# Placing split weights 4,224 bytes apart, with sets aside by 0, 64 or 96 bytes, in a one-core encoder layer

## The chip, the cores and the metric

The kernel runs on one core of one Trainium2 chip. The metric is the device time of one execution in microseconds. Three executions of the kernel before were timed; their median counts. One more execution was profiled: its trace holds the start of every instruction on each engine, the DMA packets and the semaphore events, but no addresses.

## The reference

One encoder layer over 512 positions of width 1,024, in float32:

```python
h = modulate(rmsnorm(x, norm_ffn1), sh1, sc1)
x = x + 0.5 * g1 * swiglu(h, w_ffn1_in, w_ffn1_out)      # inner width 2816
h = modulate(rmsnorm(x, norm_mix), sh2, sc2)
qa, ka, va, qb, kb, vb, ga, gb = split(h @ w_in)
ya = window_gqa_sink(rope(norm(qa)), rope(norm(ka)), va, sink_a) @ w_branch_a
yb = subln(diff_attention(rope(norm(qb)), rope(norm(kb)), vb, lam)) @ w_branch_b
x = x + g2 * ((sigmoid(ga) * ya + sigmoid(gb) * yb) @ w_out)
h = modulate(rmsnorm(x, norm_ffn2), sh3, sc3)
x = x + 0.5 * g3 * swiglu(h, w_ffn2_in, w_ffn2_out)
```

The nine vectors sh, sc and g are `silu(c) @ w_mod + b_mod`.

## The kernel before

**Precision.** Every large product is made in three matmuls of the type fp32r. Both factors are split into a high part (the value rounded to fp32r, by ScalarE) and a low part (the rest, by VectorE); `split_from` (line 190) does this. The three are high x high, high x low and low x high: `mm3` (lines 174 to 176), and `two` (lines 443 to 445), which does it for two column blocks of 256 moving columns. `first_products` (681), `project` (1125 to 1127) and `project_pairs` (1144 to 1146) issue the same three; in the last two the roles are exchanged, so that the weights are the moving operand and the hidden state is loaded into the array.

**Where weights lie.** A weight tile arrives by DMA in a `raw` tile (four buffers) and is split into a set: a high part of 128 x 1,024 in the tile `high` and a low part in the tile `low`. Each of these has five places (`HILO`) of 1,024 columns (4,096 bytes per partition); `high_low` hands them out in turn and skips those that are held. With `aside` a set begins some columns after the start of its place. Before, the columns are: 0 by default; 16 (`ASIDE`, 64 bytes) for the sets of the seven-product units (`Unit.prepare`), `project_pairs`, gate 5, two sets of `w1i`, most sets of branch A and the last two of the mix; 64 (`FAR`) for the second matmul of FFN 1 (`Out1.prepare`); 8 (`STEP`) and 56 (`STEP_1`) for one set each. A set of 1,024 columns with 16 aside reaches 16 columns into the next place. Some units keep weights elsewhere: `apart` sets in a `b8` tile, three gates in `u4` tiles.

**The moving side.** Hidden states and activations lie split in tiles `b8` (4 x 512 columns; twelve buffers) and `u4` (2 x 512; six buffers).

**Stages, in order.** (1) FFN 1 up: `first_products` with 512 moving columns, then plain pairs from `w1i`, then units of seven products instead of eight (`Unit`, a Strassen-like scheme, 256 moving columns). Four times between them `Out1` makes the second matmul for a chunk of the inner width (512 columns). (2) A boundary that makes the last four sets of `Out1` by halves of the sequence (256 columns) while the next norm is made, with three gates. (3) Projections of the two attentions, the attentions themselves, the remaining gates beside them, the two branches; branch A by halves (256 columns). (4) The mix `w_mix`: six sets with 512 columns, then two by halves. (5) FFN 2: a plain unit, then units, each two 256 wide.

**What sets the order.** In FFN 1 and FFN 2 `run_items` writes the order out, with due times for loads (`ASK`) and splits (`MAKE`), and a split is only made when a place is free. In the attentions a planner (`Line`) orders pieces by their costs. TensorE, VectorE and ScalarE follow that written order in the boundaries and in the first stage; elsewhere the framework orders them by their dependencies. Weight DMAs are issued by SyncE, additions to weights in memory (`accum_op`) by GpSimd.

**Addresses.** A tile's place in memory follows from the order in which the kernel first asks for its name; sizes are rounded up to 32 bytes. Before that order is: `half`, 24 `sm`, `ones`, `ident`, `par`, 8 `x`, `high`, six `mod`, `low`, three `mod`, `sub8`, `lam_s`, `nlam`, `begin`, `ka`, 12 `b8`, `ccol`, 6 `u4`, `pos`, 4 `raw`, 8 `f2`, then small ones up to nearly the end of the memory. `half` stands at byte 4,224.

Of the kernel before, what the change touches and what calls it, by code (L numbers as in the profile page):

```python
# [11 lines left out]
F32 = mybir.dt.float32  # L12
F32R = mybir.dt.float32r
I32 = mybir.dt.int32
# [4 lines left out]
P = 128  # L19
D = 1024  # L20
T = 512
NC = D // P
NT = T // P
# [73 lines left out]

RAW, HILO, F2 = 4, 5, 8

ASIDE = 16  # L100

FAR = 64


STEP, STEP_1 = 8, 56
BRANCH_ASIDES = (STEP, ASIDE, ASIDE, ASIDE), (ASIDE, ASIDE, 0, 0)
MIX_ASIDES = 0, 0, 0, 0, 0, 0, ASIDE, ASIDE

CHUNKS = (range(0, 6), range(6, 12), range(12, 16), range(16, 22))
PLAIN, LAST_1 = 3, 4  # L110
# [24 lines left out]
def layer(ctx: ExitStack, tc: tile.TileContext, a: dict):  # L135
# [31 lines left out]
    def keep(shape, nm, dt=F32):  # L167
        return sb.tile(shape, dt, name=nm, tag=nm, bufs=1)
# [28 lines left out]
    def high_low(n=1024, aside=0, holder=None):  # L197
        while turn[0] % HILO in holders:
            turn[0] += 1
        i = turn[0] % HILO  # L200
        turn[0] += 1
        if holder:
            holders[i] = holder
        i = i * 1024 + aside
        return tuple(t[:, i : i + n] for t in parts)

    def let_go(holder):
# [16 lines left out]
    half = keep([P, 8], "half")  # L224
    V.memset(half, -0.5)
    S.activation(small(8), half, AF.Silu)
    ones = keep([P, P], "ones")
    V.memset(ones, 1.0)
    ident = keep([P, P], "ident")
    make_identity(nc, ident)  # L230

    par = keep([P, NPAR], "par")
    x = [xt() for _ in range(NC)]
    parts, modv = [], []
    for nm, n in (("high", 6), ("low", 9)):
        parts.append(keep([P, HILO * 1024 + ASIDE], nm, F32R))
        modv += [keep([P, NC], f"mod{v}") for v in range(len(modv), n)]
    sub8, lam_s, nlam = (keep([P, n], nm) for nm, n in (("sub8", 1), ("lam_s", 2), ("nlam", 1)))

    def mod_load(v, c, w=None):  # L240
        if w is None:
# [2 lines left out]
        return w  # L244


    begin, begins, norms = keep([P, 8 * NC], "begin"), {}, {SC1: NORM1, SC2: NORM2, SC3: NORM3}

    def mod_begin(v):
        if v in (SH1, SH2, SH3):  # L250
# [33 lines left out]
    class Norm:  # L284
# [41 lines left out]
        def sums(self, sq, r, first, last):  # L326
            if first:
                self.st[r.start] = bank("op" if r.start else "tp")
            for t in range(r.start // P, r.stop // P):
                i = 2 * (t - r.start // P)  # L330
                PE.matmul(
                    self.st[r.start][:, i : i + 2], sq[:, t * P : (t + 1) * P], ones[:, 0:2],
                    start=first and i == 0, stop=last and (t + 1) * P == r.stop, skip_group_check=True,
                )

# [111 lines left out]
    class Unit:  # L447
# [12 lines left out]
        MAKE = {"s1": 5, "a11": 3, "a12": 2, "s2": 4, "s4": 2, "s3": 2, "a22": 3}  # L460
        asked, length = ("s1", "a11", "a12", "a22"), 1.0

        in_order = ()
        spare, roomy, apart, more = ("s1",), (), (), {"s1": ("s2", "a11"), "s2": ("s4", "a12"), "a11": ("s3", "a21")}

        def place(self, q):
# [14 lines left out]
        def prepare(self, q):  # L481

            if q in self.ready:
                return
            self.ask(q)
            n = self.depth * 2 * P
            if q in self.apart:
                both = b8().rearrange("p a b -> p (a b)")
                hi, lo = both[:, 0:n], both[:, 1024 : 1024 + n]
            else:  # L490
                hi, lo = high_low(n, ASIDE, (self, q))
            t = self.at[q]
            with tc.issue_after(copied[0]) if q in self.in_order and copied else nullcontext():
                split_from(hi, lo, t)
            self.ready[q] = hi, lo
            if q in self.more:
                s, src = self.more[q]
                G.dma_start(t, self.srcs[src], accum_op=ALU.add)
                self.at[s] = t
# [101 lines left out]

    cact = [sbuf("ka", [P, D], F32, 1)]
    hh, hl = new_h()
    ccol = keep([P, 3 * NC], "ccol")[:, 0:NC]
    nc.scalar.dma_start(ccol, a["c"])
    tc.keep_in_program_order(nc.scalar.dma_start(par, a["par"]))
    for c in range(NC):
# [2 lines left out]
    with tc.manual_schedule(engines=BOUND | {mybir.EngineType.SP, mybir.EngineType.Pool}):  # L610
# [14 lines left out]
                start=j == 0, stop=j == 3, skip_group_check=True,  # L625
            )
        warm(3)
        w1, pos = {}, []

        def first_loads(k):  # L630
            scale = mod_load(SC1, k)
            if k == 0:
                pos.append(keep([P, NT], "pos", I32))
            shift = mod_load(SH1, k) if k == 0 else None
            raw = sbuf("raw", [P, 1024], F32, RAW)
            nc.sync.dma_start(raw, a["w1s"][k])
            w1[k] = [scale, shift or mod_load(SH1, k), raw]
# [134 lines left out]
    rest, later, latest = rest[: EARLY * NC], rest[EARLY * NC : (EARLY + NEXT) * NC], rest[(EARLY + NEXT) * NC :]  # L772

    row = u4(F32).rearrange("p a b -> p (a b)")[:, 0:NROW]
    pos = pos[0]
    freq = keep([P, HD // 2], "freq")
    small_loads = [
        (row, a["row"].partition_broadcast(P)), (pos, a["pos"]), (freq, a["freq"].partition_broadcast(P)),
# [54 lines left out]
    class Out1:  # L833
# [17 lines left out]
        def prepare(self, m):  # L851
            if m not in self.ready:
                self.ask(m)
                aside = FAR if not self.by_halves(m) else STEP_1 if m == NC - LAST_1 else ASIDE
                if self.final and m == 0:
                    while turn[0] % HILO != 1:
                        turn[0] += 1
                t = self.ready[m] = high_low(self.depth * P, aside, (self, m))
                with tc.issue_after(copied[0]):
                    split_from(*t, self.at[m])  # L860
# [52 lines left out]
    with tc.manual_schedule(engines={mybir.EngineType.SP, mybir.EngineType.Pool}):  # L913
# [4 lines left out]
        for q in range(4, 2 * PLAIN):  # L918

            w, sums_from = loaded1, split[1]  # L920
            if q < 5:
                with tc.issue_after(split[0]), tc.issue_after(split[1]):
                    loaded1 = [load_split(a["w1i"][1, k], aside=ASIDE) for k in range(2)]
            behind = split[1]
            out = pair_banks()
            for k in range(NC):
                wh, wl = w[k // 4]
                for i in range(2):
                    o = (k % 4) * 256 + i * P
# [53 lines left out]
    V.tensor_scalar(sub8, par[:, SUBLN : SUBLN + 1], 1.0 - LAM_INIT, None, ALU.mult)  # L983

    NF = HD // 2
    posf = keep([P, NT], "posf")
    V.tensor_copy(posf, pos)
    tb = u4(F32)
    tb = [tb[:, i, :] for i in range(2)]
# [141 lines left out]
    def project_pairs(srcs, then):  # L1131

        n = 2 * P
        out = [bank("acc") for _ in range(2)]
        for u, src in enumerate(srcs):
            wh, wl = load_main(src, ASIDE)
            for t in range(NT):
                ht = slice(t * P, (t + 1) * P)
                po = out[t // 2][:, t % 2 * n : (t % 2 + 1) * n]
                for i in range(4):  # L1140
                    k = 4 * u + i
                    w = slice(i * n, (i + 1) * n)
                    first, last = k == 0 and t % 2 == 0, k == NC - 1 and t % 2 == 1
                    PE.matmul(po, hh[k][:, ht], wh[:, w], start=first, stop=False, skip_group_check=True)
                    PE.matmul(po, hh[k][:, ht], wl[:, w], start=False, stop=False, skip_group_check=True)
                    PE.matmul(po, hl[k][:, ht], wh[:, w], start=False, stop=last, skip_group_check=True)
                    yield MM3 / 2
        then(out)
# [11 lines left out]
    def gates(more=lambda: True):  # L1160
        while gate_next[0] < 16 and more():
            j = gate_next[0]
            gate_next[0] += 1

            wh, wl = load_main(a["w_gate"][j], ASIDE * (j == EARLY_A))
            out = bank("acc")
            for k in range(NC):
                o = k * P
                mm3(out, wh[:, o : o + P], wl[:, o : o + P], hh[k], hl[k], k == 0, k == NC - 1)
                yield MM3  # L1170
            gate_end(j, out)
# [71 lines left out]

    kb_h, kb_l, vb_h, vb_l, qb_h, qb_l = (b8() for _ in range(6))
    rqb = keep([P, NT, 8], "rqb")
    nrqb = keep([P, NT, 8], "nrqb")
    ob_h, ob_l = b8(), b8()
    done, turns = {"a": 0, "b": 0}, {"a": 0, "b": 0, "o": 0, "w": (0, 0), "q": 0, "t": 0}

# [143 lines left out]
    def tables_a():  # L1393
        late = u4(F32).rearrange("p a b -> p (a b)")
        nc.sync.dma_start(late, table_scr)
        table["qa"], table["ka"] = (four(late)[i : i + 2] for i in (0, 2))
        ka = sbuf("ka", [P, 2, T], F32R, 1)
        wa.update(k=(ka[:, 0, :], ka[:, 1, :]), rq=keep([P, NT, 8], "rqa"))

    def two_blocks(raw, nh, tabs, i, rs, scale8):  # L1400

# [211 lines left out]
    def main():  # L1613
# [30 lines left out]

        for i, r in enumerate(HALVES):
            line.drain(lambda: done["a"] >= 2 * i + 2)
            yield from branch(a["w_ya"], 0, *wa["o"], then_b, load_split, r, BRANCH_ASIDES[i])

    mix = []
    line.run(main())  # L1650
# [9 lines left out]
    nc.sync.dma_start(cact[0], c_scr.partition_broadcast(P))  # L1660
    mod_begin(G3)
    for m in range(NC):
        w = load_split(a["w_mix"][m], aside=MIX_ASIDES[m])

        def products(po, r, w=w):
            wh, wl = w
# [107 lines left out]
            V.scalar_tensor_tensor(g, g, -1.0, self.bank[1, t], ALU.mult, ALU.mult)  # L1774

    plain = units[0] = Plain(units[0].srcs, 4, h_operand, None, 0)
    lead = units[1]
    lead.spare, lead.roomy, lead.apart = ("s1", "a11", "a12"), ("a22",), ("s1", "a12")
    for u in units[1:]:
# [254 lines left out]
```

## Time and profile before

| | us |
|---|---|
| three timed executions | 1045.57, 1045.63, 1048.86 |
| their median | 1045.63 |
| the profiled execution | 1044.11 |
| its span, first to last instruction | 1042.3 |
| busy: matmuls (PE) | 1034.8 |
| busy: weight loads (PEld) | 953.2 |
| busy: VectorE (DVE) | 785.5 |
| busy: ScalarE (ACT) | 575.6 |
| busy: GpSimd (POOL) | 165.7 |

The ends of matmuls are modelled in the profile and overlap, so their busy time is no measure of their speed. How fast they follow each other is read from the starts in the timeline: the start of the last of a run less that of the first, by the count between them. A name such as `acc<-b,high` lists the tile that is written and the tiles that are read, buffer numbers left out (`b` is `b8`, `u` is `u4`). The granted clock of TensorE is 0.999 of full speed throughout.

### The profile page before, as it was taken

What the parts mean: (1) busy time and instruction counts of PE and PEld (TensorE: products, weight loads), DVE (VectorE), ACT (ScalarE), POOL (GpSimd) and SP (SyncE); (2) the same over time, 40 slices, a digit from 0 to 9 for tenths busy, and PEclk for the clock granted to TensorE, in tenths of its full rate; (3) what the DMA queues carried; (4) which work ended last, traced back from release to release, by engine and by line L of the source; (5) the groups of instructions that cost most, each with busy time, mean ns of one, the idle gap of its engine ahead of it and who ended that gap; (6) DMA issues with size and microseconds to landing.
All of it is one profiled execution on the core that took longest, in us unless ns stands there. A gap on an engine that the chain in (4) does not pass through costs nothing.

```text
span 1042.3 us, 18751 instructions
## 1 busy us (share of the span) xinstructions
PE 1034.8 (99%) x7348; PEld 953.2 (91%) x7348; DVE 785.5 (75%) x1436; ACT 575.6 (55%) x948; POOL 165.7 (16%) x190
## 2 busy tenths in 40 slices
PE   9999999999999999999999999999999999999998
PEld 6889899899998998899888888989999999999998
DVE  6886667567796679859772588976899777877867
ACT  6664335234454442667785855525867556655553
POOL 1101110110110100543333101001111111112110
PEclk9999999999999999999999999999999999999999
DMA  9977786966984459796646834974498998989874
GB/s 366 346 218 187 242 235 198 275 173 180 259 207 150 149 203 410 232 261 140 179 97 184 242 124 158 366 229 112 98 238 190 244 226 206 231 216 220 208 150 127
DMA packets 68793, 220.92 MB, mean 212 GB/s; under 512 B 8288, under 2 KB 10976, under 8 KB 68704
## 3 DMA queue, kind: packets, MB, share of 16 engines
q1 hardware_dynamic: 46224, 146.52, 38.7%
q0 software_dynamic: 19344, 68.70, 35.1%
q10 hardware_dynamic: 3136, 4.51, 1.2%
q8 instruction: 57, 0.93, 0.3%
q14 instruction: 32, 0.26, 0.1%
HBM read 209.46 MB, written 10.23 MB: 211 GB/s over the span
## 4 chain that ended last, share of the span: by engine, by line
PE 93%; DVE 3%; ACT 3%; issue 0%; DMA 0%; POOL 0%; DVEq 0%; ACTq 0%; POOLq 0%
PE acc L443 7%; PE acc L444 7%; PE acc L445 7%; PE sc L443 6%; PE sc L445 6%; PE sc L444 6%; PE sc L174 5%; PE sc L175 5%; PE sc L176 5%; PE acc L174 4%; PE acc L176 4%; PE acc L175 4%; PE acc L1125 2%; PE acc L1126 2%; PE acc L1127 2%; PE tp L1203 1%
## 5 line engine op out<-in xcount | busy, mean ns | idle before, releaser
L190 ACT CAST high<-raw 128x1024 fp32r<-128x1024 f32 (+2 forms) x160 | 155.9, 985 | 149.8 <-PE sc L175 37.7
L190 DVE TENSOR_TENSOR low<-raw,high 128x1024 fp32r<-128x1024 f32 (+2 forms) x160 | 181.3, 1141 | 49.4 <-ACT high L190 48.5
L443 PE MATMUL acc<-b,high 128*128 128x256 f32 x508 | 140.9, 277 | 0.0
L444 PE MATMUL acc<-b,high 128*128 128x256 f32 x508 | 140.7, 277 | 0.1
L445 PE MATMUL acc<-b,low 128*128 128x256 f32 x508 | 140.6, 277 | 0.0
L445 PE MATMUL sc<-b,low 128*128 128x256 f32 x500 | 138.5, 277 | 0.0
L443 PE MATMUL sc<-b,high 128*128 128x256 f32 x500 | 138.5, 277 | 0.0
L444 PE MATMUL sc<-b,high 128*128 128x256 f32 x500 | 138.4, 277 | 0.0
L190 DVE TENSOR_TENSOR low<-u,high 128x1024 fp32r<-128x1024 f32 (+1 forms) x73 | 87.5, 1200 | 21.8 <-ACT high L190 20.3
L190 ACT CAST high<-u 128x1024 fp32r<-128x1024 f32 (+1 forms) x73 | 75.4, 1036 | 49.1 <-PE sc L175 16.2
L174 PE MATMUL sc<-b,high 128*128 128x512 f32 (+1 forms) x272 | 97.5, 359 | 0.0
L175 PE MATMUL sc<-b,high 128*128 128x512 f32 (+1 forms) x272 | 97.3, 358 | 0.0
L176 PE MATMUL sc<-b,low 128*128 128x512 f32 (+1 forms) x272 | 97.1, 357 | 0.0
L444 PEld LDWEIGHTS acc<-b,high 128*128 128x128 f32 x508 | 95.5, 188 | 0.4 <-DVE b L1818 0.3
L443 PEld LDWEIGHTS acc<-b,high 128*128 128x128 f32 x508 | 95.5, 188 | 0.3 <-ACT f L520 0.2
L445 PEld LDWEIGHTS acc<-b,low 128*128 128x128 f32 x508 | 95.4, 188 | 0.0
L443 PEld LDWEIGHTS sc<-b,high 128*128 128x128 f32 x500 | 94.1, 188 | 0.2 <-ACT f L520 0.2
L445 PEld LDWEIGHTS sc<-b,low 128*128 128x128 f32 x500 | 93.9, 188 | 0.1
L444 PEld LDWEIGHTS sc<-b,high 128*128 128x128 f32 x500 | 93.9, 188 | 0.0
L174 PE MATMUL acc<-b,high 128*128 128x512 f32 (+1 forms) x240 | 89.4, 372 | 0.3 <-DVE u L190 0.3
L176 PE MATMUL acc<-b,low 128*128 128x512 f32 (+1 forms) x240 | 87.1, 363 | 0.0
L175 PE MATMUL acc<-b,high 128*128 128x512 f32 (+1 forms) x240 | 86.9, 362 | 0.0
(387 smaller groups left out, 2713.5 us busy)
## 6 DMA issues: line engine op xcount, KB each, us to landing
u<-w_mod SPq DMA_DIRECT2D x40, 512.0 KB, 8.0
b<-w_mod SPq DMA_DIRECT2D x32, 512.0 KB, 5.7
raw<-w2i SPq DMA_DIRECT2D x31, 512.0 KB, 5.3
u<-w2i POOLq DMA_DIRECT2D x31, 512.0 KB, 7.1
u<-w1u POOLq DMA_DIRECT2D x24, 512.0 KB, 7.4
raw<-w1u SPq DMA_DIRECT2D x24, 512.0 KB, 6.7
raw<-w1o SPq DMA_DIRECT2D x24, 384.0 KB, 4.3
raw<-w_gate SPq DMA_DIRECT2D x16, 512.0 KB, 4.2
```

The costliest lines, as they stand in the source:

```text
L174: PE.matmul(out, wh, xh, start=first, stop=False)
L175: PE.matmul(out, wh, xl, start=False, stop=False)
L176: PE.matmul(out, wl, xh, start=False, stop=last)
L190: last = S.copy(hi, src), V.tensor_tensor(lo, src, f(hi), ALU.subtract)
L443: PE.matmul(out, wh[:, s], xh, start=first and j == 0, stop=False, skip_group_check=True)
L444: PE.matmul(out, wh[:, s], xl, start=False, stop=False, skip_group_check=True)
L445: PE.matmul(out, wl[:, s], xh, start=False, stop=last and j == 1, skip_group_check=True)
L1125: PE.matmul(out[t][:, 0:n], hh[k][:, ht], wh[:, o : o + n], start=k == 0, stop=False)
L1126: PE.matmul(out[t][:, 0:n], hh[k][:, ht], wl[:, o : o + n], start=False, stop=False)
L1127: PE.matmul(out[t][:, 0:n], hl[k][:, ht], wh[:, o : o + n], start=False, stop=k == NC - 1)
L1203: PE.transpose(tp[:, j * P : (j + 1) * P], src, ident)
```

## The change

Places are 1,056 columns (`PLACE`, 4,224 bytes) apart instead of 1,024, so no set reaches into the next place. Sets stand aside by 0 columns where the moving side is 512 wide, by 16 (`NARROW`, 64 bytes) where it is 256 wide, and by 24 (`TURN`, 96 bytes) in a few sets: sets 4 and 5 of the last `Out1`, set 1 of branch A's first half, set 6 of the mix, and `a11` and `a21` of the plain unit in FFN 2. The two `w1i` sets and gate 5, with 512 moving columns, go from 16 to 0; the last two sets of branch A from 0 to 16; `Out1` from 64 to 0.

Memory is paid for elsewhere: `ones` has 2 columns instead of 128, `begin` 6 x 8 instead of 8 x 8, `ccol` 8 instead of 24; `nrqb` takes the buffer of `freq`, `rqa` that of `Ckb`. `sub8`, `lam_s`, `nlam`, `pos`, two of the `mod` tiles and `ccol` are asked for before `x`, one `mod` tile stands between `high` and `low` and three after `low`, three after `b8`. No product, split or DMA is added or taken away.

```diff
-ASIDE = 16
-FAR = 64
-STEP, STEP_1 = 8, 56
-BRANCH_ASIDES = (STEP, ASIDE, ASIDE, ASIDE), (ASIDE, ASIDE, 0, 0)
-MIX_ASIDES = 0, 0, 0, 0, 0, 0, ASIDE, ASIDE
+PLACE, NARROW, TURN = 1024 + 32, 16, 24
...
-        i = i * 1024 + aside
+        i = i * PLACE + aside
...
-    ones = keep([P, P], "ones")
+    ones = keep([P, 2], "ones")
...
+    sub8, lam_s, nlam = (keep([P, n], nm) for nm, n in (("sub8", 1), ("lam_s", 2), ("nlam", 1)))
+    pos = keep([P, NT], "pos", I32)
+    parts, modv = [], []
+    def mods(n):
+        modv.extend(keep([P, NC], f"mod{v}") for v in range(len(modv), n))
+    mods(2)
+    ccol = keep([P, NC], "ccol")
     x = [xt() for _ in range(NC)]
-    parts, modv = [], []
-    for nm, n in (("high", 6), ("low", 9)):
-        parts.append(keep([P, HILO * 1024 + ASIDE], nm, F32R))
-        modv += [keep([P, NC], f"mod{v}") for v in range(len(modv), n)]
+    for nm, n in (("high", 3), ("low", 6)):
+        parts.append(keep([P, (HILO - 1) * PLACE + 1024 + TURN], nm, F32R))
+        mods(n)
...
-    begin, begins, norms = keep([P, 8 * NC], "begin"), {}, {SC1: NORM1, SC2: NORM2, SC3: NORM3}
+    begin, begins, norms = keep([P, 6 * NC], "begin"), {}, {SC1: NORM1, SC2: NORM2, SC3: NORM3}
...
-        in_order = ()
+        in_order = turned = ()
...
-                hi, lo = high_low(n, ASIDE, (self, q))
+                hi, lo = high_low(n, TURN if q in self.turned else NARROW, (self, q))
...
-    ccol = keep([P, 3 * NC], "ccol")[:, 0:NC]
+    mods(9)
...
-                aside = FAR if not self.by_halves(m) else STEP_1 if m == NC - LAST_1 else ASIDE
+                aside = 0 if not self.by_halves(m) else TURN if m < NC - LAST_1 + 2 else NARROW
...
-                    loaded1 = [load_split(a["w1i"][1, k], aside=ASIDE) for k in range(2)]
+                    loaded1 = [load_split(a["w1i"][1, k]) for k in range(2)]
...
-            wh, wl = load_main(a["w_gate"][j], ASIDE * (j == EARLY_A))
+            wh, wl = load_main(a["w_gate"][j])
...
-    nrqb = keep([P, NT, 8], "nrqb")
+    nrqb = sbuf("freq", [P, NT, 8], F32, 1)
...
-        wa.update(k=(ka[:, 0, :], ka[:, 1, :]), rq=keep([P, NT, 8], "rqa"))
+        wa.update(k=(ka[:, 0, :], ka[:, 1, :]), rq=sbuf("Ckb", [P, NT, HD], F32, 1)[:, :, 0:8])
...
-            yield from branch(a["w_ya"], 0, *wa["o"], then_b, load_split, r, BRANCH_ASIDES[i])
+            yield from branch(a["w_ya"], 0, *wa["o"], then_b, load_split, r, [NARROW, NARROW if i else TURN, NARROW, NARROW])
...
-        w = load_split(a["w_mix"][m], aside=MIX_ASIDES[m])
+        w = load_split(a["w_mix"][m], aside=0 if m < NC - LAST else TURN if m == NC - LAST else NARROW)
...
+    plain.turned = ("a11", "a21")
```

More of the change, by code (lines that the diff above doesn't have):

```diff
@@ L232, in layer @@
     par = keep([P, NPAR], "par")
-    x = [xt() for _ in range(NC)]
-    parts, modv = [], []
-    for nm, n in (("high", 6), ("low", 9)):
-        parts.append(keep([P, HILO * 1024 + ASIDE], nm, F32R))
-        modv += [keep([P, NC], f"mod{v}") for v in range(len(modv), n)]
-    sub8, lam_s, nlam = (keep([P, n], nm) for nm, n in (("sub8", 1), ("lam_s", 2), ("nlam", 1)))
+    sub8, lam_s, nlam = (keep([P, n], nm) for nm, n in (("sub8", 1), ("lam_s", 2), ("nlam", 1)))
[5 more added lines that the diff above has]
+    ccol = keep([P, NC], "ccol")
+    x = [xt() for _ in range(NC)]
+    for nm, n in (("high", 3), ("low", 6)):
+        parts.append(keep([P, (HILO - 1) * PLACE + 1024 + TURN], nm, F32R))
+        mods(n)
     def mod_load(v, c, w=None):
@@ L331, in sums @@
                 PE.matmul(
-                    self.st[r.start][:, i : i + 2], sq[:, t * P : (t + 1) * P], ones[:, 0:2],
+                    self.st[r.start][:, i : i + 2], sq[:, t * P : (t + 1) * P], ones,
                     start=first and i == 0, stop=last and (t + 1) * P == r.stop, skip_group_check=True,
@@ L627, in layer @@
         warm(3)
-        w1, pos = {}, []
+        w1, kept = {}, []
         def first_loads(k):
@@ L632, in first_loads @@
             if k == 0:
-                pos.append(keep([P, NT], "pos", I32))
+                kept.append(keep([P, NT], "posf"))
             shift = mod_load(SH1, k) if k == 0 else None
@@ L774, in layer @@
     row = u4(F32).rearrange("p a b -> p (a b)")[:, 0:NROW]
-    pos = pos[0]
     freq = keep([P, HD // 2], "freq")
@@ L985, in layer @@
     NF = HD // 2
-    posf = keep([P, NT], "posf")
+    posf = kept[0]
     V.tensor_copy(posf, pos)
@@ L1135, in project_pairs @@
         for u, src in enumerate(srcs):
-            wh, wl = load_main(src, ASIDE)
+            wh, wl = load_main(src, NARROW)
             for t in range(NT):
```

## The prediction

> **What bounds the kernel now.** I read the page from its top first: the span, the busy time of each engine and the granted clock, then the chain that ended last.
>
> ```profile
> span 1042.3 us, 18751 instructions
> PE 1034.8 (99%) x7348; PEld 953.2 (91%) x7348; DVE 785.5 (75%) x1436; ACT 575.6 (55%) x948; POOL 165.7 (16%) x190
> PEclk9999999999999999999999999999999999999999
> PE 93%; DVE 3%; ACT 3%; issue 0%; DMA 0%; POOL 0%; DVEq 0%; ACTq 0%; POOLq 0%
> ```
>
> TensorE is the bound from end to end and its clock is never cut, so the time can only move with the distance from one matmul's start to the next one's (the pitch). The chip waits next to nothing: this is the whole list of PE's waits.
>
> ```profile
> PE acc L617 <- POOL ident masks.py:199: 1.3, 1, 1.3
> PE acc L681 <- ACT b L669: 0.4, 2, 0.2
> PE op L331 <- ACT f L292: 0.3, 1, 0.3
> PE acc L174 <- DVE u L190: 0.3, 1, 0.3
> ```
>
> That is 2.3 us, 1.3 of it at the start. Whatever the change saves in waits is inside this. Next the groups by line and shape, for the counts. Each group but those of line 681 stands for one of the three products of a set (high x high, high x low, low x high: lines 443, 444, 445, or 174, 175, 176, or 1125 to 1127), and the other two have the same counts.
>
> ```profile
> L443 PE MATMUL acc<-b,high 128*128 128x256 f32 x508 | 140.9, 277 | 0.0
> L443 PE MATMUL sc<-b,high 128*128 128x256 f32 x500 | 138.5, 277 | 0.0
> L443 PE MATMUL op<-b,high 128*128 128x256 f32 x94 | 26.0, 277 | 0.0
> L443 PE MATMUL tp<-b,high 128*128 128x256 f32 x94 | 26.0, 276 | 0.0
> L174 PE MATMUL sc<-b,high 128*128 128x512 f32 x192 | 74.8, 390 | 0.0
> L174 PE MATMUL acc<-b,high 128*128 128x512 f32 x176 | 71.3, 405 | 0.3 <-DVE u L190 0.3
> L1125 PE MATMUL acc<-high,b 128*128 128x512 f32 x72 | 28.3, 393 | 0.0
> L1125 PE MATMUL sc<-high,b 128*128 128x512 f32 x24 | 9.4, 390 | 0.0
> L681 PE MATMUL acc<-b,high 128*128 128x512 f32 x45 | 17.7, 392 | 0.2 <-ACT b L669 0.2
> L681 PE MATMUL sc<-b,high 128*128 128x512 f32 x45 | 17.5, 390 | 0.0
> ```
>
> So 1,196 x 3 = 3,588 matmuls are 256 wide with weights in a place and a `b8` tile moving. The 277 ns are modelled ends; the pitch has to be taken from starts. The timeline gives them; its columns are start, duration, engine, line, operation. I quote the first start of a run of equal matmuls and the start that ends it.
>
> ```profile
> 801.27 0.28 PE L443 MATMUL acc<-b,high 128*128 128x256 f32 x1
> 817.59 0.28 PE L443 MATMUL acc<-b,high 128*128 128x256 f32 x1
> ...
> 651.25 0.28 PE L174 MATMUL acc<-b,high 128*128 128x256 f32 x1
> 665.39 0.28 PE L174 MATMUL acc<-b,high 128*128 128x256 f32 x1
> 671.15 0.40 PE L174 MATMUL sc<-b,high 128*128 128x512 f32 x1
> ...
> 734.78 0.28 PE L443 MATMUL sc<-b,high 128*128 128x256 f32 x1
> 746.09 0.28 PE L443 MATMUL tp<-u,b 128*128 128x256 f32 x1
> ...
> 455.71 0.28 PE L1144 MATMUL acc<-high,b 128*128 128x256 f32 x1
> 463.37 0.28 PE L1146 MATMUL acc<-high,b 128*128 128x256 f32 x1
> ...
> 891.34 0.28 PE L443 MATMUL sc<-u,high 128*128 128x256 f32 x1
> 894.14 0.28 PE L443 MATMUL acc<-b,high 128*128 128x256 f32 x1
> 894.50 0.28 PE L443 MATMUL acc<-b,high 128*128 128x256 f32 x1
> ...
> 364.81 0.36 PE L174 MATMUL acc<-b,u 128*128 128x256 f32 x1
> 377.60 0.28 PE L176 MATMUL acc<-b,u 128*128 128x256 f32 x1
> ...
> 682.05 0.39 PE L174 MATMUL sc<-b,high 128*128 128x512 f32 x1
> 703.59 0.39 PE L176 MATMUL sc<-b,low 128*128 128x512 f32 x1
> ...
> 71.36 0.40 PE L174 MATMUL acc<-b,high 128*128 128x512 f32 x1
> 82.33 0.39 PE L176 MATMUL sc<-b,low 128*128 128x512 f32 x1
> ```
>
> To sort these I need addresses, which the trace lacks. They follow from the order in which the kernel first asks for its tiles, each rounded up to 32 bytes: before, `high` starts at byte 22,848, `low` at 43,584, `b8` at 68,672, all 64 beyond a multiple of 256, and `u4` is 160 beyond one. Places are 4,096 bytes apart, so a set standing aside by a bytes has the offset (moving minus weight address, modulo 256) of -a against `b8`, in both of its halves. Then:
>
> - 256 wide, offset 192 (aside 64): 144 matmuls from 801.27 at 16.32/144 = 113.3 ns; but 120 from 651.25 and 96 from 734.78 at 117.8. Same offset, two speeds, each held for as long as nothing disturbs it: a lock that is caught or missed at the entry.
> - 256 wide, offset 0: 48 from 665.39, 120.0 ns.
> - offset 32 (`u4` moving): 24 from 891.34, 116.7 ns; after it the fast lock is back within three matmuls (894.14 to 894.50 is 0.36 us for three, then 0.113 each).
> - offset 64 (place moving, `b8` as weights): 65 from 455.71, 117.8 ns.
> - offset 160 (`u4` as weights): 107 from 364.81, 119.5 ns.
> - 512 wide, offset 0: 95 from 682.05, 226.7 ns; offset 192 (aside 64): 47 from 71.36, 233.4 ns.
>
> The pitch thus depends on the offset, and by opposite rules for the two widths.
>
> **The change part by part.** After it the order of tiles puts `high` at 22,592 (again 64 beyond), `low` at 43,712 (192 beyond), `b8` at 69,184 and `u4` at 167,584 (as before modulo 256). `ones` (512 bytes to 32) and a smaller `begin` and `ccol` pay for it.
>
> *Places 4,224 bytes apart.* This is 128 modulo 256. Place i of `high` moves by 128 i, place i of `low` by 128 + 128 i. So in every set one half keeps its offset and the other moves by 128: `low` in places 0, 2, 4, `high` in places 1, 3. With two loads of `high` to one of `low`, a third of the loads move in even places and two thirds in odd ones: 0.6/3 + 0.4 x 2/3 = 47% of all. For the 256-wide sets the moved loads go from offset 192 to 64; for the 512-wide from 0 to 128.
>
> Offset 64 is in the trace: 117.8 ns, never the fast lock, in all 65 of that run. Some 3,250 of the 3,588 matmuls are locked now (the rest stands in runs like that of 734.78). Upper bound, if no lock survives: 3,250 x (117.8 - 113.3) = 14.5 us. Lower bound, if only the moved loads pay: 47%, 6.8 us. I take the even places at the lower end and the odd ones at the upper, since a lock needs three quiet matmuls (894.14 to 894.50) and odd places have two moved loads in three: 14.5 x (0.6/3 + 0.4) = 8.7 us.
>
> Offset 128 for 512 wide is nowhere in the trace. Some 1,480 matmuls (3 x (192 + 176 + 72 + 24), and 90 of line 681), 47% of them moved: between 0 (like offset 0) and 696 x 6.7 = 4.7 us (like 192, the nearest row). A gain is excluded, as they run at the fastest pitch seen. Since what is dear at one width is free at the other, neither row is a safe guide: I take half, 2.3 us.
>
> *Sets put right.* The two `w1i` sets of line 922 go from aside 64 to 0: 48 x 6.7 = 0.3 us less; gate 5 likewise, 24 x 6.7 = 0.2 us. Together 0.5 us saved, for the half that isn't moved surely.
>
> *Sets that turn (96 bytes).* They replace 224 bytes in the first split set of FFN 1 and 32 in the first of branch A, and are new for set 6 of the mix and two of the plain unit. Offset 160, and 32 in the moved half. Their own pitch (119.5 and 116.7 by the rows above) is within 0.1 us of now. If they catch the lock, the run of 120 above and the 48 at 120.0 (now aside 64) gain 120 x 4.5 + 48 x 6.7 = 0.9 us; the 96 from 734.78 follow a set of `b8` weights, at which no turning set stands. In my case there is no lasting lock to catch: 0, at best -0.9.
>
> *No overlap.* Before, a set aside by 64 bytes reached into the next place, so ScalarE and VectorE splits had to wait for products of the neighbour. These waits are hidden behind TensorE: the four PE waits leave at most 0.3 us that could be one of them. 0.
>
> *Moved small tiles.* `nrqb` now takes the place of `freq`, `rqa` that of `Ckb`, `posf` and `pos` are asked for earlier. VectorE writes them long after the last reader of the old tile; cover: 99% busy PE, cost if gone: one wait of the size seen, 0.3 us. `ones` is set in 2 columns for 128. `ident` moves by 32 bytes modulo 256 as the moving side of transposes. 0 each, within 0.3. No DMA is added or moved past a queue.
>
> Sum: 8.7 + 2.3 - 0.5 = +10.5 us. The profiled execution took 1044.11 us (span 1042.3 and 1.8 around it), so 1054.6 against it; the median of the runs is 1045.63, 1.5 above, so 1056.1 us.
>
> **The rivals.**
>
> *The period is 128 bytes, not 256* (other side). Then moving by 128 is invisible, all offsets are what they were, the two wrong widths are put right and the turning sets work: -0.5 - 0.9 = -1.4 us, 1044.2. It decides from the point where offsets 64 and 192 behave alike. For it: no row has the same pair of tiles 128 apart. Against it: 64 (117.8) and 192 (113.3) are 128 apart, and so are 32 (116.7) and 160 (119.5). It could be rescued if the role (place moving, `b8` loaded) made the first pair slow, and the company of other work the second. Other slow entries that then catch the lock would carry it beyond -3.1.
>
> *Addresses don't matter at all* and the pitches come from the stages they lie in: 1045.6. For it only that each offset lies in few stages. Against it the step from 117.8 to 120.0 at 665.39 and back from 116.7 to 113.3 at 894.5, inside one stage, with nothing changed but the set. The Trainium skill ("SBUF — State Buffer", "Who interferes with whom") gives PE two independent read ports and says that PE waits for nobody; by that rule this rival would hold. The trace disagrees: 113.3 against 120.0 ns for one shape at a full clock.
>
> *Both widths pay in full*: 14.5 + 4.7 - 0.5 = +18.7, 1064.3. For it the 65 of 455.71 that never lock; against it that the unmoved loads keep the good offset.
>
> **How the numbers follow.** 0.3% (3.1 us) is about what a measurement here can tell from no change. Forecast 0.60 (own range 1050 to 1062), in full 0.06, period of 128 0.28, no effect 0.06. The first two are slower: 0.66. Of the period of 128 I give 0.15 to more than 3.1 us saved and 0.13 to less, so faster 0.15, same 0.19. The range leaves out a tenth at each end: 1042.3 to 1063.
>
> **What would show it.** Right: runs of lines 443 to 445 at 116 to 118 ns with odd places worse than even, and lines 174 to 176 above 226.7 in half of the loads. Wrong: 113.3 in places 1 and 3 as in 0, 2, 4, with 651 to 671 now at 113.3 too; then the period is 128. The two `w1i` sets near 71 should fall from 233.4 in any case but the second rival's.

## The result, and the profile after

The changed kernel is slower: 1051.95 us in the median (1050.55 to 1055.48) against 1048.2 us for the kernel before, timed beside it. The ratio is 1.0043, with a 95% interval of 1.0029 to 1.0057. Forecast were 1056.1 us and a range of 1042.3 to 1063.0. So the direction and the range held, but the parts of the sum did not, as the traces show.

The profiled execution took 1053.95 us, 9.84 above the one before. Its page, the rows that answer to those of before (the last is the whole list of TensorE's longer waits):

```profile
span 1052.2 us, 18744 instructions
PE 1044.6 (99%) x7348; PEld 958.0 (91%) x7348; DVE 784.8 (75%) x1436; ACT 576.5 (55%) x948; POOL 165.9 (16%) x190
PEclk8999999999999999999999999999999999999999
```

```profile
PE acc L617 <- POOL ident masks.py:199: 1.4, 1, 1.4
PE sc L443 <- ACT f L520: 0.6, 1, 0.6
PE op L331 <- ACT f L292: 0.3, 1, 0.3
PE acc L167 <- DVE u L183: 0.2, 1, 0.2
```

TensorE is still the bound and still waits for almost nothing, 2.5 us in place of 2.3. The clock row differs in its first digit. By stretches of the span (busy time of each engine, then the granted clock), first after, then before:

```profile
0.00:26.00 26.00, 24.65 (x105) 19.41 (x106) 14.88 (x35) 14.13 (x25) 3.72 (x9) 0.87 0.95 358
```

```profile
0.00:26.00 26.00, 24.21 (x116) 17.71 (x117) 17.47 (x40) 16.77 (x28) 4.24 (x10) 1.00 0.96 366
```

The 0.87 is a mean. The drop itself is shorter, to about half of the clock for 7 us (after):

```profile
13.50:20.60 7.10, 7.10 (x34) 6.76 (x34) 4.08 (x10) 3.75 (x8) 2.01 (x3) 0.53 1.03 412
```

The first hundred matmuls lose 2.8 us by it, and nothing after them. Without it the profiled difference is 7.0 us. Executions with a mean clock of 0.997 or less take about 3 us longer than those at 0.999 and above, with every kernel here (the kernel before 1048.5 against 1045.6 us in its next series, the changed one 1054.5 against 1051.5), so the two kernels differ by 5.9 us at a full clock, where the medians, in which both kinds are mixed, differ by 3.75.

The starts tell where these 7 us lie. The timeline after, first the stretch of branch A and of the mix that the prediction read at 651 to 704 us (lines 167 to 169 are 174 to 176 of before):

```profile
663.21 0.28 PE L167 MATMUL acc<-b,high 128*128 128x256 f32 x1
674.09 0.33 PE L167 MATMUL acc<-b,high 128*128 128x256 f32 x1
...
690.77 0.39 PE L167 MATMUL sc<-b,high 128*128 128x512 f32 x1
...
701.87 0.40 PE L167 MATMUL sc<-b,high 128*128 128x512 f32 x1
...
707.48 0.39 PE L167 MATMUL sc<-b,high 128*128 128x512 f32 x1
...
74.82 0.39 PE L167 MATMUL acc<-b,high 128*128 128x512 f32 x1
85.98 0.28 PE L443 MATMUL sc<-u,high 128*128 128x256 f32 x1
```

From 663.21 to 674.09 lie 96 matmuls of 256 columns in places 1 to 4: 113.3 ns, odd places as even ones, where before this stretch had 117.8. From 690.77 lie two 512-wide sets in even places (48 matmuls): 231.3 ns. The next one, in place 1 (24 from 701.87), has 233.8. Before, all of these had 226.7. The two `w1i` sets (48 from 74.82) have 232.5, before 233.4.

For a balance I worked out every pitch from the starts, sorted by the addresses (as in the prediction), and summed what lies above the fastest pitch (113.3 ns, or 226.7). Pitches over 128 or 256 ns are left out; these are waits, or lie where the clock dropped.

| delay, us | before | after |
|---|---|---|
| 512 wide, all loads | 1.7 | 8.1 |
| of these, offset 0 | 1.3 (1,506 loads) | 3.4 (840) |
| of these, offset 128 | none | 4.7 (738) |
| 256 wide, sets 64 bytes aside | 3.1 | 1.8 |
| 256 wide, all other sets in a place | 2.3 | 3.5 |
| `project_pairs` | 1.2 | 1.2 |

The whole loss is in the 512-wide products: +6.4 us. The 256-wide ones, which should have lost 8.7, end where they were. With 0.2 us more of waits that is 6.5 of the 7.0 us; the rest I can't place.

### The profile page after: what moved, and what is told of

Read it like the earlier page. It is cut to its first block, busy times and chain, and to the rows that moved or that the text cites. A ratio compares the mean times of both kernels' runs of the same rounds, so it can differ in the third digit from the quotient of the medians.

```text
span 1052.2 us, 18744 instructions
## 1 busy us (share of the span) xinstructions
PE 1044.6 (99%) x7348; PEld 958.0 (91%) x7348; DVE 784.8 (75%) x1436; ACT 576.5 (55%) x948; POOL 165.9 (16%) x190
## 4 chain that ended last, share of the span: by engine, by line
PE 92%; ACT 3%; DVE 3%; DMA 1%; issue 1%; POOL 0%; ACTq 0%; DVEq 0%; POOLq 0%
PE acc L444 6%; PE acc L443 6%; PE acc L445 6%; PE sc L443 6%; PE sc L445 6%; PE sc L444 6%; PE sc L169 5%; PE sc L168 5%; PE sc L167 5%; PE acc L167 5%; PE acc L168 5%; PE acc L169 5%; PE acc L681 2%; PE sc L681 2%; PE acc L1124 2%; PE acc L1125 2%
## 5 line engine op out<-in xcount | busy, mean ns | idle before, releaser
L183 DVE TENSOR_TENSOR low<-u,high 128x1024 fp32r<-128x1024 f32 (+1 forms) x73 | 87.5, 1200 | 21.3 <-ACT high L183 19.9
```

Source lines behind the costliest of these rows:

```text
L183: last = S.copy(hi, src), V.tensor_tensor(lo, src, f(hi), ALU.subtract)
```

## The experiments

**Theory A**: a 512-wide product wants offset 0 modulo 256 in both halves; 256-wide ones repeat every 128 bytes. **Theory B**, that of the prediction: both repeat every 256 bytes only. **Theory C**: not the offset, but the spacing or the other moved tiles.

### One half moved, and both

In the kernel before, places 4,096 bytes apart, only the order of small tiles is edited:

```diff
-    for nm, n in (("high", 6), ("low", 9)):
+    for nm, n in (("high", 2), ("low", 9)):      # low128: four mod tiles go behind low
```

For `both128`, `sub8`, `lam_s`, `nlam` and one `mod` stand ahead of `high`, for `high128` the same with two `mod` tiles between the halves instead of six. Below, (192, 64) stands for offset 192 in `high` and 64 in `low`.

> The kernel before, with its places 4,096 bytes apart, and only the tile `low` moved by 128 modulo 256 (four of the small `mod` tiles stand behind it instead of ahead of it); the same instructions. Every set then looks like one of an even place of the changed kernel. Theory A (512-wide loads want offset 0 modulo 256, 256-wide ones repeat every 128): the 512-wide sets of lines 174 to 176 run 227, 232, 234 ns in turn, 231 in the mean, so some 1,578 matmuls x 4.3 ns = +6.8 us, ratio 1.0065; the 256-wide runs keep 113.3 ns. Theory B, that of the prediction (256-wide loads repeat only every 256): besides, a third of 3,250 matmuls at 117.8 in place of 113.3, +4.9 us more, 1.011. Theory C (the 4,224-byte spacing or the other moved tiles made the 231 ns, not the offset): 226.7 stays, ratio 1.000.

> The kernel before with both `high` and `low` moved by 128 modulo 256, so that all 512-wide products of line 174 to 176 have offset 128 in both halves and all 256-wide ones offset 64 in place of 192; the same instructions, places 4,096 apart. If offset 128 itself is what a 512-wide load pays for: 233 ns throughout, 1,578 x 6.7 = +10.6 us, ratio 1.010. If it is the mixture of two offsets in one set that costs: 226.7 stays, ratio 1.000. Theory B (256-wide loads repeat only every 256): all 3,250 locked matmuls of 256 columns go to 117.8, +14.5 us, 1.014 with 512-wide ones free, 1.024 with them at 233. Theory A has 113.3 for the 256-wide ones in any case.

> The kernel before with only `high` moved by 128 modulo 256 (places 4,096 apart): every set then looks like one of an odd place of the changed kernel. With `low` moved alone it was 1.0034 (512-wide sum of delays +5.7 us, 256-wide 113.5 ns), with both moved 1.019 (512-wide 232.6 ns, 256-wide 117.6 ns). If a 256-wide set needs one half at offset 192 and doesn't care which (theory A2): 113.5 to 114 ns here too, -1 us; 512-wide as in the odd places of the changed kernel, 233, 232, 235 ns in turn, 1,578 x 6.7 = +10.6 us; ratio 1.009. If the first two loads of a triple decide, they are at 64 here, as in the kernel with both moved: 117.6 ns, +14 us besides, ratio 1.022. If each load pays for its own offset: two thirds of what both together paid, 1.013.

Measured: `low128` 1049.13 us, ratio 1.0034 (1.0022 to 1.0047). `both128` 1066.42 us, 1.019 (1.0177 to 1.0203). `high128` 1059.65 us, 1.0123 (1.0108 to 1.0139). The timeline of `low128`, of `both128` and of `high128`:

```profile
656.41 0.28 PE L174 MATMUL acc<-b,high 128*128 128x256 f32 x1
659.17 0.28 PE L174 MATMUL acc<-b,high 128*128 128x256 f32 x1
670.05 0.34 PE L174 MATMUL acc<-b,high 128*128 128x256 f32 x1
...
681.40 0.39 PE L174 MATMUL sc<-b,high 128*128 128x512 f32 x1
...
703.59 0.39 PE L174 MATMUL sc<-b,high 128*128 128x512 f32 x1
```

```profile
688.58 0.39 PE L174 MATMUL sc<-b,high 128*128 128x512 f32 x1
...
710.89 0.39 PE L174 MATMUL sc<-b,high 128*128 128x512 f32 x1
...
815.71 0.28 PE L443 MATMUL acc<-b,high 128*128 128x256 f32 x1
...
841.15 0.28 PE L443 MATMUL acc<-b,high 128*128 128x256 f32 x1
```

```profile
174.04 0.28 PE L443 MATMUL sc<-b,high 128*128 128x256 f32 x1
...
182.60 0.28 PE L443 MATMUL op<-b,high 128*128 128x256 f32 x1
...
811.82 0.28 PE L443 MATMUL acc<-b,high 128*128 128x256 f32 x1
...
836.29 0.28 PE L443 MATMUL acc<-b,high 128*128 128x256 f32 x1
```

512 wide: 96 matmuls of `low128` from 681.40 take 231.1 ns each, 96 of `both128` from 688.58 take 232.4. So Theory C is out, as the spacing is 4,096 here, and offset 128 costs by itself, without any mixture.

256 wide: (64, 64) in `both128` runs at 117.8 ns through 216 matmuls from 815.71, and nearly everywhere else. That is Theory B, and Theory A is wrong there. (192, 64) in `low128` has 115.0 in its first set (24 from 656.41) and 113.3 in the next four, and needs no more than one set for it nearly everywhere. (64, 192) in `high128` does both: 118.9 through three sets from 174.04, 113.3 through nine from 811.82. It stays at the speed at which it was entered.

How often is a 256-wide set at the fast speed? Of 187 unbroken stretches of one set (9 matmuls or more; some 160 of them at the offsets named), these have a mean under 114 ns:

| kernel | offsets of the sets 64 bytes aside | fast stretches |
|---|---|---|
| before | (192, 192) | 127 |
| `low128` | (192, 64) | 148 |
| `high128` | (64, 192) | 62 |
| `both128` | (64, 64) | 5 |
| after | in turn (192, 64) and (64, 192) | 131 |

Summed as above, `low128` gains 1.6 us in its 256-wide sets and loses 5.7 in its 512-wide products, +4.1; measured +3.6. `both128` loses 14.1 and 7.1, +20.6 with 0.6 gained in `project_pairs`; measured +19.9. `high128` loses 9.4 and 6.9, +16.3; its profiled span is 15.8 longer, its ratio says +12.9. The sum for `high128` holds for the profiled execution, then, and 3 us of it stay unexplained in the median. Its ratio is that of the expectation by which each load pays for its own offset (1.013), but that mechanism isn't there: it would give one pitch, and of the 164 stretches at (64, 192) 62 are under 114 ns and 90 at 118 to 119. **Theory A3** follows for 256 columns: (192, 64) finds the fast speed by itself, (192, 192) and (64, 192) keep the speed that they are given, and (64, 64) has no fast one.

### The spacing undone, and the 512-wide loads put right

```diff
-PLACE, NARROW, TURN = 1024 + 32, 16, 24
+PLACE, NARROW, TURN = 1024, 16, 24               # place1024
...
```

```diff
-        i = i * PLACE + aside
-        return tuple(t[:, i : i + n] for t in parts)
+        at = [i * PLACE + aside] * 2             # fix
+        if not aside:
+            at[(i + 1) % 2] += 32
+        return tuple(t[:, j : j + n] for t, j in zip(parts, at))
...
```

The rest of both edits moves small tiles or adds pads, so that `high`, `low` and `b8` stand as the expectations say.

> The changed kernel with places 4,096 bytes apart again (a set that stands aside overlaps its neighbour by 64 or 96 bytes, as before the change), small pads keeping `high`, `low` and `b8` all 64 beyond a multiple of 256; the new asides and turning sets stay. Theory A: the 512-wide loads are at 226.7 again, 6.4 us less than the changed kernel, and the cleaner locks of its 256-wide sets stay: about 1.9 us under the kernel before, ratio 0.998. If the moved small tiles or the turning sets cost the time: it stays above the kernel before, about 1.004.

> The changed kernel, places 4,224 bytes apart and none overlapping, but sets that don't stand aside have their `high` half 128 bytes further in odd places and their `low` half 128 bytes further in even ones, so that every 512-wide load has offset 0 modulo 256; the 256-wide asides stay as they are, at offsets 192 and 64. Theory A: 226.7 ns in lines 167 to 169, 6.4 us less than the changed kernel, ratio to the kernel before 0.998. Theory B would keep half of the 256-wide loads at 117.8, but the changed kernel's trace has 113.3 there, so it can't. If the spacing costs by something else than the offset: no better than the changed kernel, 1.004.

`place1024` took 1055.21 us, 1.0085 (1.0069 to 1.0102), much worse than either forecast. In it the last columns of a set that stands aside are overwritten by the next set, so part of the products are of other weights. Its 512-wide products are at 226.7 again (delay 1.3 us), so that part of the forecast held. Much of the time went into waits, 9.9 us in all. Here are three of them, then a split ahead of the first, then the busy times and the clock around it:

```profile
PE sc L167 <- ACT high L183: 3.5, 1, 3.5
PE acc L167 <- ACT high L183: 1.2, 1, 1.2
PE acc L169 <- DMA low<-w_gate: 0.9, 1, 0.9
```

```profile
676.87 1.04 ACT L183 CAST high<-raw 128x1024 fp32r<-128x1024 f32 x1 [1.30 <-DMA raw<-w_mix]
```

```profile
675.00:690.00 15.00, 11.53 (x45) 9.29 (x44) 7.50 (x15) 5.03 (x8) 0.00 (x0) 0.77 0.75 260
```

TensorE waits for splits into `high`. Before the longest wait ScalarE itself had waited for the load of `w_mix`, not for a product of the neighbouring place, so that the overlap causes these waits is not shown; where the delay began stays open. At the end of that wait the granted clock fell, to a mean of 0.77 from 675 to 690 us, and the 512-wide matmuls from 680.55 to 684.39 followed each other every 427 ns; the sum of the waits leaves this out. This run says nothing about the small tiles.

`fix` took 1047.19 us, 1.001 (0.9997 to 1.0022). Its timeline:

```profile
73.83 0.39 PE L167 MATMUL acc<-b,high 128*128 128x512 f32 x1
84.70 0.28 PE L446 MATMUL sc<-u,high 128*128 128x256 f32 x1
...
679.93 0.39 PE L167 MATMUL sc<-b,high 128*128 128x512 f32 x1
...
701.69 0.39 PE L167 MATMUL sc<-b,high 128*128 128x512 f32 x1
```

The `w1i` sets (48 from 73.83) are at 226.5 ns, the mix (96 from 679.93) at 226.7. The 512-wide delay falls from 8.1 to 1.2 us with nothing else changed, and the busy time of TensorE from 1044.6 to 1037.6 us, both with the drop of the clock at the start. That settles where the loss came from. Against the kernel before I expected 0.998, which failed: by the balance `fix` has 0.7 us less delay than the kernel before (512-wide products 1.2 against 1.7 us, 256-wide sets 5.2 against 5.4) and waits 1.0 us more (3.3 against 2.3), so there was no gain to be had.

### The pitch by itself

`pitch_table` and `pitch_scan` run only sets of triples from `high` and `low` against a fixed `moving` tile, each set at its own aside. The name of a result tells columns and asides: `q256h64l192e` is 256 wide, with `high` 64 and `low` 192 bytes aside, so offsets (192, 64). A name with `e` in place of `q` is a set by which the next one is entered.

> Nothing of the layer is computed: the four input blocks are copied to SBUF once, the output is filled with raw input, and TensorE runs sets of triples (high x a, high x b, low x a) of one shape with weights at a known offset to a fixed moving tile, first with all else idle, each set twice in two orders, then with VectorE and ScalarE copying beside. Theory A2 at 256 columns: 113.3 ns with offset 192 in both halves and with 192 and 64 mixed either way, 117.6 with 64 in both, 120 at 0. At 512 columns: 226.7 at 0, 233 at 192, 231 to 233 at 128 in both or one half. If the pitches come from the other engines' traffic and not from the offset: 113.3 and 226.7 in all sets while all else is idle.

> Nothing of the layer is computed; sets of triples as in the table of pitches, for all 64 pairs of asides of `high` and `low` in steps of 32 bytes. At 256 columns each pair is entered twice: from a slow set (offset 0 in both halves, 120 ns) and from a fast one (offset 192 in `high`, 64 in `low`, 113.3 ns). At 512 columns each pair once. Theory A3 (a set of `high` at 192 and `low` at 64 catches the fast lock by itself; 192 in both, and 64 in `high` with 192 in `low`, only keep a lock that they find; 64 in both has none): behind the slow set 113.3 for the first alone and about 117.8 for the other three, behind the fast set 113.3 for the first three and 117.8 for 64 in both. If there are no two stable speeds: the same pitch behind both entries in every pair. At 512 columns 226.7 for 0 in both and nowhere else.

Two stretches of `pitch_table` by engine (PE, PEld, DVE, ACT, POOL busy, then the clock), one with all else idle and one with both other engines copying, and the first starts of some sets:

```profile
40.00:300.00 260.00, 260.00 (x2210) 259.92 (x2210) 0.00 (x0) 0.00 (x0) 0.00 (x0) 1.00 0.00 1
...
580.00:690.00 110.00, 110.00 (x934) 110.00 (x933) 71.39 (x168) 100.15 (x166) 0.00 (x0) 1.00 0.01 1
```

```profile
51.19 0.28 PE L86 MATMUL q256h64l64e<-moving,high 128*128 128x256 f32 x1
...
62.50 0.28 PE L86 MATMUL q256h96l96e<-moving,high 128*128 128x256 f32 x1
...
344.08 0.39 PE L86 MATMUL q512h128l128e<-moving,high 128*128 128x512 f32 x1
...
355.24 0.40 PE L86 MATMUL q512h160l160e<-moving,high 128*128 128x512 f32 x1
...
388.63 0.39 PE L86 MATMUL q512h0l128e<-moving,high 128*128 128x512 f32 x1
...
399.73 0.40 PE L86 MATMUL q512h128l0e<-moving,high 128*128 128x512 f32 x1
```

At 256 columns: (192, 192), 96 matmuls from 51.19, 117.8 ns behind a set at offset 224. At 512 columns, 48 matmuls each: (128, 128) 232.5, (0, 128) 231.3. With ScalarE busy for 91% and VectorE for 65% of the time, each set has the settled pitch that it had in one of its two turns with all else idle, within 0.05 ns. So the traffic of other engines is not the cause. The Trainium skill ("SBUF — State Buffer", "Who interferes with whom") says that PE waits for no other engine, and this agrees. It also calls PE's two read ports, for the moving operand and for weights, independent. Here, with nothing else running, the pitch of one shape goes from 113.3 to 120.0 ns by the distance of these two operands alone; the measurement decides.

It is the distance of the two operands that counts and not the address of either. By the order of tiles `moving` stands 128 bytes beyond a multiple of 256 here, `b8` 64 beyond one in the layer; a weight 128 beyond a multiple has 226.7 ns at 512 columns here (offset 0) and 233.4 in the layer (offset 192, the `w1i` sets before).

`pitch_scan` enters each pair of asides once from a slow set (offset 0, 120 ns) and once from a fast one. The first start of a set and the first of the set behind it, 48 matmuls later:

```profile
220.78 0.28 PE L81 MATMUL q256h64l192e<-moving,high 128*128 128x256 f32 x1
226.23 0.28 PE L81 MATMUL e256h0l0e<-moving,high 128*128 128x256 f32 x1
...
494.18 0.28 PE L81 MATMUL q256h192l192e<-moving,high 128*128 128x256 f32 x1
499.83 0.28 PE L81 MATMUL e256h0l0e<-moving,high 128*128 128x256 f32 x1
...
1033.68 0.28 PE L81 MATMUL q256h192l192e<-moving,high 128*128 128x256 f32 x1
1039.12 0.28 PE L81 MATMUL e256h64l192e<-moving,high 128*128 128x256 f32 x1
```

(192, 64) from the slow set: 113.5 ns. (64, 64) from the slow set: 117.7, and from the fast one: 113.3. One pair of offsets, two speeds, by the entry alone: that is the lock, shown. Six other pairs settle more than 1 ns apart by the entry too, and (128, 64) the other way round: 116.7 ns behind the slow set, 120.0 behind the fast one. Of all 64 pairs only the four made of 64 and 192 reach 113.3; the rest stay between 115.5 and 124.4 ns. At 512 columns only (0, 0) reaches 226.7; the other 63 lie between 228.7 and 235.6.

A3 is right in kind and too simple in detail. It had (64, 64) without a fast speed, and (192, 192) and (64, 192) slow behind the slow set; both were fast at once behind that one (offset 0), while behind offset 224 (192, 192) was not, and in `high128` (64, 192) stayed at 118.9. Which entry lets which pair in is not a rule that I can state.

### Sets with sums in `u4`, turning sets, and `u4` itself

The set of a unit's product `s1` (an s1 set below) has, in most units, a sum as its moving operand, which lies in a `u4` tile.

```diff
-high_low(n, TURN if q in self.turned else NARROW, (self, q))
+high_low(n, TURN if q in self.turned else 8 if q == "s1" else NARROW, (self, q))   # s1_8, on fix
...
-PLACE, NARROW, TURN = 1024 + 32, 16, 24
+PLACE, NARROW, TURN = 1024 + 32, 16, 16                                            # s1_8_no_turn, on s1_8
```

> The kernel with every 512-wide load at offset 0 (ratio to the kernel before 1.001), and besides the s1 sets, whose moving operand is a `u4` tile 160 beyond a multiple of 256, stand 32 bytes aside in place of 64: offsets 64 in one half and 192 in the other, for 160 and 32. By theory A2 their 456 matmuls go from 118.3 ns in the mean to 113.7: -2.1 us, ratio 0.999. If the sets are slow for what runs beside them and not for the offset: 1.001 again.

> The same, and the sets that turn (96 bytes aside, 240 matmuls at 119 ns) stand aside by 64 bytes like the others. If a turning set is what lets the sets after it catch the fast lock: its own 240 x 5.5 = 1.3 us are saved, but long runs behind 512-wide products stay at 117.8, 120 to 400 matmuls x 4.5 = 0.5 to 1.8 us lost: within 0.5 us of the kernel with turning sets. If the mixture of 192 and 64 locks by itself: 1.3 us saved, ratio 0.998, and 113.3 ns right behind the 512-wide products.

`s1_8`: 1047.94 us, 1.0 (0.9986 to 1.0014). `s1_8_no_turn`: 1046.01 us, 0.9988 (0.9975 to 1.0). The first expectation failed: the delay of the 256-wide sets stayed at 5.3 us. Sorted by addresses, the s1 sets with sums in `u4` save 1.0 us, all of it in odd places, where they are now (192, 64) and have 113.6 ns for 118.9; in even ones, at (64, 192), they stay slow, 118.1 for 117.7. As much is lost elsewhere: 0.7 us in those s1 sets whose operand lies in `b8`, which this edit puts at (224, 96) or (96, 224), and most of the rest in other sets at (192, 64). Without turning sets the delay falls to 3.9 us, and the sets behind 512-wide products lock all the same: the first behind the mix has 113.7 ns, the next 113.3. The turning sets are not needed for the lock where the halves are mixed; they cost their own 119 ns.

In `u4_128`, on top of this, `u4` moves by 32 bytes, s1 sets with sums in `u4` start at the very beginning of their place, and s1 sets with a `b8` operand go back to 64 bytes:

```diff
-high_low(n, TURN if q in self.turned else 8 if q == "s1" else NARROW, (self, q))
+high_low(n, None if q == "s1" and self.sums_in_u4 else NARROW, (self, q))
...
-    mods(9)
+    mods(8)                                       # the ninth is asked for behind freq
```

> The kernel with 512-wide loads at offset 0 and no turning sets (ratio to the kernel before 0.9988), and `u4` is moved by 32 bytes, to 128 beyond a multiple of 256, so that an s1 set with sums in `u4` stands at the very start of its place with offsets 64 and 192, an s1 set with its operand in `b8` stands aside by 64 bytes like the others, and products between `u4` and `b8` themselves have offset 64 or 192 in place of 96 or 160. If these offsets lock wherever the table has 113.3 ns: the s1 sets of the last stage with `b8` operand, 96 matmuls at 118.3, save 0.4 us, the products between `u4` and `b8` (384 at about 119) up to 2 us, ratio 0.997. If those products are paced by what they wait for and not by the offset, 0.3 to 0.5 us: 0.9985.

1044.73 us against 1047.73 beside it, ratio 0.9969 (0.9953 to 0.9985): this beats both kernels. The delay of the 256-wide sets in places is 1.9 us (5.4 before the change) and that of the 256-wide products with weights in `u4` or `b8` 1.4 (2.3). 144 of 187 stretches are fast. It is bought with a little more waiting, 5.3 us in all, so there is something left.

## Why the prediction was right, and where not

- *What bounds the kernel*: right. Nothing but the pitch and the clock of the first 26 us moved.
- *The lock, caught or missed at the entry*: right, and shown by the scan with one pair of offsets at both speeds.
- *Moved 256-wide loads, +8.7 us, in bounds of 6.8 to 14.5*: this step failed. It measured -1.3 us (3.1 to 1.8), and the sign that the prediction names for being wrong was there: 113.3 ns in odd places as in even ones. The upper bound was nearly right for what it described, all loads at offset 64: `both128` lost 14.1. The step from there to a mixture was wrong: I let each moved load pay for itself and break the lock for its neighbours, and held 64 for an offset that never locks, where (64, 64) is fast behind a fast set in the scan. The row for it came from `project_pairs`, 65 matmuls with exchanged roles. What counts is the pair of offsets in the set and the speed at which it is entered. The places in turn lock at least as well as 192 alone (131 fast stretches against 127), though (64, 192) throughout does not (62).
- *Moved 512-wide loads, +2.3, in bounds of 0 to 4.7*: the mechanism was right and the size too small; +6.4 us was measured. The upper bound was no bound, because only the moved loads paid in it (and 1,480 loads were counted where there are 1,578: 90 of the 186 of line 681). The unmoved ones beside them lost as well: 840 of them have 3.4 us, where at the rate of before (1.3 us for 1,506) they would have 0.7. That is 2.7 of the 6.4 us, as in the sequence 227, 232, 234 ns of an even place, which `low128` has throughout.
- *Sets put right, -0.5*: failed. I said that the half that isn't moved would gain surely; the `w1i` sets went from 233.4 to 232.5 ns, because one half at 128 is enough to slow the set. `fix` has them at 226.5.
- *Turning sets, 0, at best -0.9*: the stretch that I named did gain, about 0.7 us by its pitches (96 matmuls by 4.4 ns, 24 by 3.7 and 24 by 6.7). But it was the mixture that caught the lock, not the turn: `s1_8_no_turn` has it without one. The rise of 1.2 us in the other sets of the table above is what the turning sets and the s1 sets at (32, 160) pay.
- *No overlap, 0*: right for this pair of kernels, as far as the waits show it: 2.3 us with the overlap, 2.5 without. `place1024`, which overlaps with the new asides, waits 6.6 us more than `fix`; that the overlap is the cause is not shown.
- *Small tiles, 0, within 0.3*: no loss can be seen beyond one wait of 0.6 us for a ScalarE copy, which I can't assign to any part of the change.
- *The rivals*: a period of 128 holds for no width by itself: `both128` refutes it at 256 columns, and all 512-wide rows do. In this kernel it looked true at 256 columns, because the places alternate; the prediction was wrong to take 113.3 in all places as its sign. No effect of addresses and both widths in full are out, the latter because it had no sum for mixtures either.

That the time lay within the range is luck, then: a loss forecast in the 256-wide products, which didn't come, stood in for what was forecast too small in the 512-wide ones.

## What to carry to other kernels

When every matmul loads its weights and the pitch sets the time, sort the pitches by the distance of moving and weight operand modulo 256 before moving anything, and keep the whole sequence of distances in view: the neighbours in a set pay too. A spacing that is odd in units of 128 bytes moves one half, high or low, of every set; keep it a multiple of 256 for products that want one distance, or shift the halves separately as `fix` does. A price for one load taken out of a row with other roles or another entry is no price: measure the sequence alone, from a slow and from a fast entry.

## What the runs showed of the hardware that I had not expected

- Two stable speeds for one sequence of fp32r matmuls, 113.3 and 117.8 ns at 256 columns, chosen by what ran just before, with no other engine working.
- Which pair is fast depends on the entry in both directions: (64, 64) settles at 113.3 ns behind a fast set and 117.8 behind a slow one, (128, 64) at 120.0 and 116.7.
- The granted clock can drop to about half for some 7 us: 0.53 from 13.5 to 20.6 us in the changed kernel's profiled execution, and in `place1024` at the end of a wait of 3.5 us (matmuls 427 ns apart in place of 227).
- 4 of 64 pairs of offsets at 256 columns (one of them only behind a fast set), and 1 of 64 at 512, reach the fastest pitch; the worst pairs cost 10% (124.4 ns) and 4% (235.6 ns).
- The unmoved load in a mixed set pays as well: (0, 128) at 512 columns has 231.1 ns in the mean with one load in three off zero.
- Which read waits for which inside TensorE, and why 64 and 192 are the good distances, no run here shows; that stays open.
